# A hybrid recurrent decoder layer: the samples' queries times their states in four array columns side by side, the residual's norm moved into the second MLP product, and a third weight buffer

## The chip, the cores and the metric

One core of one Trainium2 chip runs the whole layer. The metric is the device time of one execution in microseconds. Three runs of the kernel before took 936.66, 937.22 and 938.57 us; the median is 937.22 us.

## The reference

One layer is applied to a prompt of 512 tokens and to eight samples of four tokens each, with shared weights; together they are 544 token columns. The kernel keeps activations transposed: a channel is a partition, a token a column.

```
proj = x @ w_in + b_in                       # 1024 -> 51 blocks of 128 channels
GLA:   S_t = diag(exp g_t) S_{t-1} + k_t^T v_t,  o_t = q_t S_t,   RMS norm per head, times silu(gr)
mLSTM: C_t = f C_{t-1} + i k_t v_t^T,  n_t likewise,  h_t = q_t C_t / max(|q_t . n_t|, 1),  layer norm per head
HGRN2: the same scan as GLA, with its own gate
merged = sum over branches of sigmoid(mg) * (h_branch @ w_up)
x = LayerNorm(ALPHA * x + merged @ w_out)
x = LayerNorm(ALPHA * x + square(relu(x @ w_ff_up)) @ w_ff_down)
```

The prompt starts from zero states. Each sample starts from a state that is given (for GLA and HGRN2 four heads of 48 x 96 or 64 x 64, for mLSTM four heads of 96 x 97 with n as the last column), so each sample needs its queries times its state, and its updated state goes out.

## The kernel before, in words

**Dense products.** Every dense product goes through `gemm` (L162): one block of 128 output channels by 544 tokens. A float32 weight tile `raw` is loaded on SP's queue (three buffers, L137); `wload` then splits it on ScalarE into a rounded high half `wh` (L141) and on VectorE into the rest `wl` (L142), two buffers each. `mm` (L158) issues, for each block of 128 input channels, three products (high by high, high by low, low by high) in two halves of 272 tokens: six matmuls. A product with 1024 input channels has 48 matmuls, `wup_ml` and `wup_gla` have 18, `wup_hg` 12. Its result is in one of two PSUM buffers `g` and is read by one VectorE instruction.

**Order.** A scheduler places all instructions of the program on the engines' in-order queues by a simulated time; `tc.high_priority` moves some forward. The order on each engine is therefore fixed in the built program, and the scans are mixed with the dense products: projection blocks, mLSTM (five chunks, the samples among them), GLA scan, mLSTM's merge, HGRN2 scan, the other merges, `wout` with the first norm, and the MLP in two halves of 16 hidden blocks.

**The samples' products.** In `gated` (GLA and HGRN2) `sample` makes the output transposed, `oT` (value channels by tokens). Four matmuls add the part within the four tokens (L498). For each pair of heads p and each sample n, one matmul has the state `Ss[:, n]` (128 x 96 or 128 x 64) as the stationary operand and eight columns of queries `qx` as the moving one (L509): 16 in GLA, 16 in HGRN2. They carry a lowered priority (`BEHIND`), so the scheduler puts them between other matmuls. The result is copied by ScalarE (L525), turned by four transposes (L528) and normed by `rms_rows`. In `ml_chunk(4)` the same is done for mLSTM: for each head eight matmuls with the state `Cs[:, n]` (96 x 97) stationary and four columns of queries moving (L770), 32 in all, then a copy (L781), four transposes (L784) and a copy into `num` (L785). After its products a state is scaled and updated in place (L517 to L519; L772 to L777) and stored.

A float32 matmul is two MATMUL records in the trace, each with a weight load of its own; the rounded `fp32r` ones of the dense products are one.

**The residual's norm.** The first layer norm leaves the sums `ne` (minus the mean) and `rstd` (L990 to L999); the first MLP product takes the centred but not yet normed rows and corrects its result by `ne` and `rstd` (L1037, L1038), then applies relu and square on ScalarE and splits the hidden block into high and low (L180). The residual itself, `x1`, is normed during the first 16 hidden blocks: for block m the loop issues one VectorE instruction on row block m // 2, an add of `ne` (L1052) for even m, a multiply by `rstd` (L1054) for odd m, and then an affine step on ScalarE (L1055). The second product of the first half adds its result to ALPHA times that row block.

**The last merge** (`Merge` with `wup_hg`, 2 input blocks): for each of eight output blocks a gate product of 48 matmuls is followed by an up product of 12.

Of the kernel before, what the change touches and what calls it, by code (L numbers as in the profile page):

```python
# [27 lines left out]
BEHIND = 380  # L28
# [15 lines left out]
def build(tc, I, O):  # L44
    nc = tc.nc
    with ExitStack() as ctx:
# [85 lines left out]

        def wload(src, nk):

            n = nk * 128
            raw = wp.tile([128, 1024], F32, tag="raw", name="raw", bufs=3)
            nc.sync.dma_start(out=raw[:, 0:n], in_=src)  # L137
            h = wp.tile([128, 1024], F32R, tag="wh", name="wh")
            l = wp.tile([128, 1024], F32R, tag="wl", name="wl")
            with tc.high_priority(OFF):  # L140
                nc.scalar.activation(out=h[:, 0:n], in_=raw[:, 0:n], func=AF.Copy)  # L141
                nc.vector.tensor_tensor(out=l[:, 0:n], in0=raw[:, 0:n], in1=h[:, 0:n].bitcast(F32), op=ALU.subtract)  # L142
            return h, l
# [207 lines left out]
        def gated(q, k, b, sc, dv, vtok, sname, nt, gate):  # L351
# [5 lines left out]
            def levels(u):  # L357
# [85 lines left out]
                qx = t1.tile([128, 2, 8, 2, 4], F32, tag="qx", name="qx", bufs=1)  # L443
                nc.gpsimd.memset(qx, 0.0)
                for e in range(2):
                    s = slice(64 * e, 64 * e + 64)
                    nc.vector.tensor_tensor(
                        out=qx[s, :, :, e, :], in0=qv[s].rearrange("p a (n m) -> p a n m", m=4),
                        in1=P[s, :, 0:32].rearrange("p a (n m) -> p a n m", m=4), op=ALU.mult)
# [44 lines left out]
            def sample():  # L494
                at, P, qx, k3 = (st[2][n] for n in ("at", "P", "qx", "k3"))
                oT = psr.tile([128, 512], F32, tag="r", name="oTs")
                for h in range(4):
                    nc.tensor.matmul(oT[0:dv, h * 32:(h + 1) * 32], vtok[0:32, 4, h * dv:(h + 1) * dv], at[0:32, h, 0:32],  # L498
                                     start=(h == 0), stop=False)
                v3 = stack_v(vtok[0:32, 4, 0:d4], d4)  # L500
                nb = 512 // dv // 4 * 4
                yield
                for p in range(2):
                    Ss = t1.tile([128, 8, 97], F32, tag="Ss", name="Ss")
                    nc.scalar.dma_start(out=Ss[:, :, 0:dv], in_=I[sname][p])
                    for n in range(8):

                        with tc.high_priority(-(BEHIND + 4 * n)):
                            nc.tensor.matmul(  # L509
                                oT[0:dv, p * 64:(p + 1) * 64].rearrange("p (a b) -> p a b", a=2)[:, :, 4 * n:4 * n + 4],  # L510
                                Ss[:, n, 0:dv], qx[:, p, n], start=False, stop=(p == 1 and n == 7))
# [12 lines left out]
                oTs = t1.tile([97, 128], F32, tag="oTs", name="oTsb", bufs=1)  # L524
                nc.scalar.activation(out=oTs[0:dv], in_=oT[0:dv, 0:128], func=AF.Copy)  # L525
                o = psr.tile([128, 512], F32, tag="r", name="osm")
                for h in range(4):
                    nc.tensor.transpose(o[0:32, h * dv:(h + 1) * dv], oTs[0:dv, h * 32:(h + 1) * 32], ident[0:dv, 0:dv])  # L528
                on = rms_rows(32, o[0:32, 0:d4].rearrange("p (a b) -> p a b", a=4), dv)
                yield  # L530
                finish_rows(32, on, nt, gate, TP)
# [161 lines left out]
        def ml_chunk(c):  # L693
# [53 lines left out]
            else:  # L747
# [4 lines left out]
                for h in range(4):  # L752
                    nc.vector.tensor_tensor(out=qF[h], in0=ip[0:96, h * 32:(h + 1) * 32], in1=qF[h], op=ALU.mult)
                ca = t1.tile([96, 4, 8], F32, tag="cas", name="cas", bufs=1)
                nc.vector.tensor_copy(ca[:, :, :, None], ip[0:96, 0:128].rearrange("p (h n m) -> p h n m", h=4, m=4)[:, :, :, 3:4])
                oT = psr.tile([128, 512], F32, tag="r", name="oTm")
                for h in range(4):
                    nc.tensor.matmul(oT[0:97, h * 32:(h + 1) * 32], mvt[0:32, 4, h, :], A[0:32, h * 32:(h + 1) * 32], start=(h == 0), stop=False)
# [5 lines left out]
                for h in range(4):  # L764
# [4 lines left out]
                    for n in range(8):  # L769
                        nc.tensor.matmul(oT[0:97, h * 32 + 4 * n:h * 32 + 4 * n + 4], Cs[:, n, :], qF[h][:, 4 * n:4 * n + 4],  # L770
                                         start=False, stop=(h == 3 and n == 7))
# [8 lines left out]
                oTs = t1.tile([97, 128], F32, tag="oTs", name="oTm", bufs=1)  # L780
                nc.scalar.activation(out=oTs, in_=oT[0:97, 0:128], func=AF.Copy)  # L781
                op = psr.tile([128, 512], F32, tag="r", name="opm")
                for h in range(4):
                    nc.tensor.transpose(op[0:32, h * 97:(h + 1) * 97], oTs[:, h * 32:(h + 1) * 32], ident[0:97, 0:97])  # L784
                nc.vector.tensor_copy(num[0:32], h4(op[0:32, 0:388], 97))  # L785
# [25 lines left out]
        mls.close()  # L811

# [76 lines left out]
        merged = mgp.tile([128, KD, T], F32, name="merged")  # L889
        mm_ = Merge(1, mgate, 3, "wup_ml", first=True)  # L890
# [137 lines left out]
        for blk in range(2):  # L1028
            hid = []
            deep = [hl3("hdh", "hh"), hl3("hdl", "hl")] + [w6.tile([128, 3 * T], F32R, tag="w6", name="hdw").rearrange("p (a b) -> p a b", a=3) for i in range(2)]  # L1030
            for m in range(16):
# [16 lines left out]
                if blk == 0:  # L1048

                    y = x1[:, m // 2, :]  # L1050
                    if m % 2 == 0:
                        nc.vector.tensor_tensor(out=y, in0=y, in1=ne, op=ALU.add)  # L1052
                    else:
                        nc.vector.tensor_tensor(out=y, in0=y, in1=rstd, op=ALU.mult)  # L1054
# [62 lines left out]
        hls.close()  # L1117
        gbs.close()
# [117 lines left out]
```

## Time and profile before

| what | before |
|---|---|
| time of the profiled execution | 937.23 us |
| its span, from first to last instruction | 935.1 us |
| median of three runs | 937.22 us |
| TensorE busy | 915.1 us (98%), 7271 matmul records |
| VectorE busy | 570.4 us (61%) |
| ScalarE busy | 436.9 us (47%) |
| GpSimd busy | 46.8 us (5%) |
| granted TensorE clock | 0.995 |

Some 2.1 us of the profiled time lie outside the span. The profile is one execution on the chip. A busy TensorE is one that has a matmul under way; since matmuls overlap, the time between the starts of two tells more than the duration of one. In a timeline row the first column is the start in us, the second the length of the merged piece, and x8 counts the records in it; a matmul's shape is given as stationary (128\*96) and moving (128x8). "idle before" is the time in which the engine did nothing, with the instruction that ended it. The chain of waits follows the execution back from its last instruction, at each step to what released it.

### The profile page before, as it was taken

To read this page: it belongs to the slowest core of one execution; us is meant where nothing else is said; L and a number is where in the kernel's file an instruction comes from. 1 tells how busy PE (TensorE), PEld (TensorE's weight loads), DVE (VectorE), ACT (ScalarE), POOL (GpSimd) and SP (SyncE) were. 2 spreads that over 40 slices of the span, in tenths; PEclk is the share of its full clock that TensorE was granted. 3 is DMA by queue.
4 is the path that set the end of the run, shared out by engine and by line. 5 is a ranking of instruction groups with operands and counts; after the bars stand their busy time and mean duration, and the time that the engine had idled before them with its cause. 6 is when DMAs were issued, how large, how long until landed. Compare 5 with 4: busy or idle time off the path is not lost.

```text
span 935.1 us, 17425 instructions
## 1 busy us (share of the span) xinstructions
PE 915.1 (98%) x7271; PEld 897.1 (96%) x7271; DVE 570.4 (61%) x995; ACT 436.9 (47%) x822; POOL 46.8 (5%) x62
## 2 busy tenths in 40 slices
PE   9999999999999999999999989999999999999995
PEld 7998999999999989999999989999999999999994
DVE  5886468867877658785558695553222455545345
ACT  5395222975536755535444375542111355432215
POOL 1302130001001001000000000000000000000000
PEclk9999999999999999999999999999999999999998
DMA  7321232123122113023235222222222222322302
GB/s 265 122 71 66 72 114 73 37 82 100 63 93 94 54 29 119 27 79 107 68 118 149 99 71 88 91 91 90 91 86 79 86 91 91 91 90 81 100 23 96
DMA packets 37598, 82.73 MB, mean 88 GB/s; under 512 B 12708, under 2 KB 18340, under 8 KB 37520
## 3 DMA queue, kind: packets, MB, share of 16 engines
q1 hardware_dynamic: 25072, 73.28, 24.1%
q10 hardware_dynamic: 12384, 8.33, 3.1%
q8 instruction: 57, 0.93, 0.4%
q14 instruction: 21, 0.17, 0.1%
q0 software_dynamic: 64, 0.02, 0.0%
HBM read 76.51 MB, written 5.09 MB: 87 GB/s over the span
## 4 chain that ended last, share of the span: by engine, by line
PE 93%; DVE 4%; ACT 2%; DMA 1%; issue 1%; ACTq 0%; DVEq 0%
PE g L158 79%; PE lv L410 3%; PE g L84 3%; DVE wl L142 1%; PE o L467 1%; PE qkp L682 1%; PE oTs L509 1%; ACT wh L141 1%; PE oTm L770 1%; DVE merged L1054 1%; PE oT L286 0%; PE vt L259 0%; PE o L470 0%; DMA fw<-in_wfirst 0%; DVE merged L1052 0%
## 5 line engine op out<-in xcount | busy, mean ns | idle before, releaser
L141 ACT ACTIVATE wh<-raw 128x1024 fp32r<-128x1024 f32 (+2 forms) x139 | 133.3, 959 | 231.9 <-PE g L158 199.4
L142 DVE TENSOR_TENSOR wl<-raw,wh 128x1024 fp32r<-128x1024 f32 (+2 forms) x139 | 155.2, 1117 | 134.9 <-ACT wh L141 133.1
L158 PE MATMUL g<-xh,wl 128*128 128x272 f32 x752 | 161.9, 293 | 1.2 <-DVE wl L142 1.2
L158 PE MATMUL g<-xh,wh 128*128 128x272 f32 x752 | 161.0, 293 | 0.3 <-DVE z L833 0.3
L158 PE MATMUL g<-xl,wh 128*128 128x272 f32 x752 | 160.8, 292 | 0.0
L158 PEld LDWEIGHTS g<-xh,wl 128*128 128x128 f32 x752 | 119.4, 189 | 2.9 <-DVE wl L142 2.5
L158 PEld LDWEIGHTS g<-xh,wh 128*128 128x128 f32 x752 | 119.6, 189 | 1.5 <-DVE z L833 0.5
L158 PEld LDWEIGHTS g<-xl,wh 128*128 128x128 f32 x752 | 119.4, 189 | 1.0 <-issue 0.5
L158 PE MATMUL g<-x1h,wh 128*128 128x272 f32 (+1 forms) x512 | 106.5, 289 | 2.8 <-DVE relu L1037 2.8
L158 PE MATMUL g<-x1l,wh 128*128 128x272 f32 (+1 forms) x512 | 106.5, 289 | 0.0
L158 PE MATMUL g<-x1h,wl 128*128 128x272 f32 (+1 forms) x512 | 106.3, 289 | 0.0
L158 PEld LDWEIGHTS g<-x1h,wh 128*128 128x128 f32 x512 | 80.9, 189 | 3.3 <-DVE relu L1037 3.2
L158 PEld LDWEIGHTS g<-x1l,wh 128*128 128x128 f32 x512 | 81.2, 189 | 0.1
L158 PEld LDWEIGHTS g<-x1h,wl 128*128 128x128 f32 x512 | 80.9, 189 | 0.0
L1039 ACT ACTIVATE relu<-relu,gw 128x544 f32<-128x544 f32 x32 | 24.0, 750 | 73.8 <-DVE relu L1038 73.8
L158 PE MATMUL g<-hidh,wh 128*128 128x272 f32 x280 | 58.1, 288 | 0.0
L158 PE MATMUL g<-hidl,wh 128*128 128x272 f32 x280 | 58.1, 289 | 0.0
L158 PE MATMUL g<-hidh,wl 128*128 128x272 f32 x280 | 57.9, 288 | 0.0
L158 PEld LDWEIGHTS g<-hidh,wl 128*128 128x128 f32 x280 | 43.9, 188 | 0.1
L158 PEld LDWEIGHTS g<-hidl,wh 128*128 128x128 f32 x280 | 43.9, 188 | 0.0
L158 PEld LDWEIGHTS g<-hidh,wh 128*128 128x128 f32 x280 | 43.8, 188 | 0.0
L215 DVE TENSOR_SCALAR gb<-g,vec 128x544 f32<-128x544 f32 x24 | 18.8, 783 | 31.5 <-PE g L158 31.3
(398 smaller groups left out, 1661.0 us busy)
## 6 DMA issues: line engine op xcount, KB each, us to landing
raw<-in_wff SPq DMA_DIRECT2D x64, 512.0 KB, 3.5
raw<-in_win SPq DMA_DIRECT2D x47, 512.0 KB, 3.2
xr<-in_xT SPq DMA_DIRECT2D x16, 272.0 KB, 3.4
raw<-in_wout SPq DMA_DIRECT2D x8, 512.0 KB, 3.7
out_yT<-merged SPq DMA_DIRECT2D x8, 272.0 KB, 2.2
fw<-in_wfirst ACTq DMA_DIRECT2D x8, 256.0 KB, 5.4
raw<-in_wup_ml SPq DMA_DIRECT2D x8, 192.0 KB, 2.3
raw<-in_wup_gla SPq DMA_DIRECT2D x8, 192.0 KB, 2.3
```

What stands on the lines that cost most here:

```text
L84: nc.tensor.matmul(first_ps[i][hf], w[:, i * 128:(i + 1) * 128], a[:, k, hf * HT:(hf + 1) * HT], start=(k == 0 and n == 0), stop=(k == KD ...
L141: nc.scalar.activation(out=h[:, 0:n], in_=raw[:, 0:n], func=AF.Copy)
L142: nc.vector.tensor_tensor(out=l[:, 0:n], in0=raw[:, 0:n], in1=h[:, 0:n].bitcast(F32), op=ALU.subtract)
L158: nc.tensor.matmul(ps[:, hf, 0:w_], w, a(k)[:, hf * HT:hf * HT + w_], start=(k == 0 and s == 0), stop=(k == nk - 1 and s == 2))
L215: nc.vector.tensor_scalar(out, ps, vcol(col), XMIN, ALU.add, ALU.max)
L410: nc.tensor.matmul(lv[0:R, o:o + 2 * H].rearrange("p (a b) -> p a b", a=2), Kv[:, p, c * R:(c + 1) * R], Q[:, p, :, c * H:(c + 1) * H], st ...
L467: nc.tensor.matmul(o[:, h * dv:(h + 1) * dv], at[:, c * 4 + h, :], vtok[:, cc, h * dv:(h + 1) * dv], start=(h == 0), stop=(cc == 0 and h = ...
L509: nc.tensor.matmul(oT[0:dv, p * 64:(p + 1) * 64].rearrange("p (a b) -> p a b", a=2)[:, :, 4 * n:4 * n + 4], Ss[:, n, 0:dv], qx[:, p, n], s ...
L682: nc.tensor.matmul(ps[0:96, hf, 0:HT], w[:, i, h, :], a[h][:, hf * HT:(hf + 1) * HT], start=(n == 0), stop=(n == 2))
L770: nc.tensor.matmul(oT[0:97, h * 32 + 4 * n:h * 32 + 4 * n + 4], Cs[:, n, :], qF[h][:, 4 * n:4 * n + 4], start=False, stop=(h == 3 and n == 7))
L1039: nc.scalar.activation(out=r_, in_=r_, func=AF.Relu, bias=gw[:, 1:2])
L1054: nc.vector.tensor_tensor(out=y, in0=y, in1=rstd, op=ALU.mult)
```

## The change

Three things are changed.

1. **The samples' products.** The operands are exchanged: the queries are stationary and the state is the moving operand. For GLA and HGRN2 `qx` holds for each pair of heads and each sample a block of 32 columns, zero but for the eight of this sample (two heads by four tokens, at a place that depends on whether the sample's number is even or odd); sample n = 2j + i writes to PSUM partitions 32j to 32j + 31, that is to a quarter j of the array's columns, and the two samples of a quarter are added there. In each group of eight matmuls the four quarters follow each other. mLSTM does the same with `qz`, 32 columns per sample of which four are filled, one group of eight per head. The number of these matmuls stays (16, 16 and 32); the order numbers and the lowered priority `BEHIND` are gone. The part within the four tokens now has the attention block stationary (32 x 32) and the values moving (L504, L771 of the new file), four matmuls as before, into a PSUM tile of its own that is copied at once. The result no longer needs transposes. Instead ScalarE copies it to SBUF (`oxs`), small DMAs on SP's queue bring each quarter's eight rows together (`orow`: four copies for mLSTM, eight for GLA, eight for HGRN2), and one VectorE add joins the two parts.
2. **The residual's norm.** It is taken out of the loop over hidden blocks. Before each of the eight second products of the first half, two VectorE instructions and one on ScalarE now make the normed row block in a tile of its own, `xn` (one buffer), which the product's result is added to.
3. **A third weight buffer.** From mLSTM's merge on, every third weight tile takes `wh` and `wl` from a second pool with one buffer of each (`w3`).

```diff
+        more_w, nload = [], [0]
         def wload(src, nk):
...
-            h = wp.tile([128, 1024], F32R, tag="wh", name="wh")
-            l = wp.tile([128, 1024], F32R, tag="wl", name="wl")
+            w_ = more_w[0] if more_w and nload[0] % 3 == 2 else wp
+            nload[0] += 1
+            h = w_.tile([128, 1024], F32R, tag="wh", name="wh")
+            l = w_.tile([128, 1024], F32R, tag="wl", name="wl")
...
-                oT = psr.tile([128, 512], F32, tag="r", name="oTs")
+                ol = psr.tile([128, 512], F32, tag="r", name="ol")
                 for h in range(4):
-                    nc.tensor.matmul(oT[0:dv, h * 32:(h + 1) * 32], vtok[0:32, 4, h * dv:(h + 1) * dv], at[0:32, h, 0:32],
-                                     start=(h == 0), stop=False)
+                    nc.tensor.matmul(ol[0:32, h * dv:(h + 1) * dv], at[0:32, h, 0:32], vtok[0:32, 4, h * dv:(h + 1) * dv],
+                                     start=(h == 0), stop=(h == 3))
+                os_ = tile2([32, d4], "os")
+                nc.scalar.activation(out=os_, in_=ol[0:32, 0:d4], func=AF.Copy)
...
-                    for n in range(8):
-                        with tc.high_priority(-(BEHIND + 4 * n)):
-                            nc.tensor.matmul(
-                                oT[0:dv, p * 64:(p + 1) * 64].rearrange("p (a b) -> p a b", a=2)[:, :, 4 * n:4 * n + 4],
-                                Ss[:, n, 0:dv], qx[:, p, n], start=False, stop=(p == 1 and n == 7))
+                    for i in range(2):
+                        for j in range(4):
+                            nc.tensor.matmul(ox[32 * j:32 * j + 32, p * dv:(p + 1) * dv], qx[:, p, j, i], Ss[:, 2 * j + i, 0:dv],
+                                             start=(p == 0 and i == 0), stop=(p == 1 and i == 1))
...
-                oTs = t1.tile([97, 128], F32, tag="oTs", name="oTsb", bufs=1)
-                nc.scalar.activation(out=oTs[0:dv], in_=oT[0:dv, 0:128], func=AF.Copy)
-                o = psr.tile([128, 512], F32, tag="r", name="osm")
-                for h in range(4):
-                    nc.tensor.transpose(o[0:32, h * dv:(h + 1) * dv], oTs[0:dv, h * 32:(h + 1) * 32], ident[0:dv, 0:dv])
-                on = rms_rows(32, o[0:32, 0:d4].rearrange("p (a b) -> p a b", a=4), dv)
+                oxs, orow = tile2([128, 2 * dv], "oxs"), tile2([32, d4], "orow")
+                nc.scalar.activation(out=oxs, in_=ox[:, 0:2 * dv], func=AF.Copy)
+                for j in range(4):
+                    for e in range(2):
+                        nc.sync.dma_start(out=orow[8 * j:8 * j + 8].rearrange("t (p e d) -> t p e d", p=2, e=2)[:, :, e],
+                                          in_=oxs[32 * j + 8 * e:32 * j + 8 * e + 8].rearrange("t (p d) -> t p d", p=2))
+                nc.vector.tensor_tensor(out=os_, in0=os_, in1=orow, op=ALU.add)
+                on = rms_rows(32, os_.rearrange("p (a b) -> p a b", a=4), dv)
...
-                    for n in range(8):
-                        nc.tensor.matmul(oT[0:97, h * 32 + 4 * n:h * 32 + 4 * n + 4], Cs[:, n, :], qF[h][:, 4 * n:4 * n + 4],
-                                         start=False, stop=(h == 3 and n == 7))
+                    z = qz[:, h % 2]
+                    nc.vector.tensor_copy(z.rearrange("p (n t) -> p n t", t=36)[:, :, 0:4], qF[h].rearrange("p (n m) -> p n m", m=4))
+                    for i in range(2):
+                        for j in range(4):
+                            n = 2 * j + i
+                            nc.tensor.matmul(ox[32 * j:32 * j + 32, h * 97:(h + 1) * 97], z[:, 32 * n:32 * n + 32], Cs[:, n, :],
+                                             start=(h == 0 and i == 0), stop=(h == 3 and i == 1))
...
+        w3s, w3p = pool("w3")
...
+        more_w.append(w3p)
         mm_ = Merge(1, mgate, 3, "wup_ml", first=True)
...
-                if blk == 0:
-                    y = x1[:, m // 2, :]
-                    if m % 2 == 0:
-                        nc.vector.tensor_tensor(out=y, in0=y, in1=ne, op=ALU.add)
-                    else:
-                        nc.vector.tensor_tensor(out=y, in0=y, in1=rstd, op=ALU.mult)
-                        nc.scalar.activation(out=y, in_=y, func=AF.Identity, scale=vcol(V_L1G + m // 2), bias=vcol(V_L1B + m // 2))
...
+                if blk == 0:
+                    xn = fp.tile([128, T], F32, tag="xn", name="xn", bufs=1)
+                    nc.vector.tensor_tensor(out=xn, in0=x1[:, m, :], in1=ne, op=ALU.add)
+                    nc.vector.tensor_tensor(out=xn, in0=xn, in1=rstd, op=ALU.mult)
+                    nc.scalar.activation(out=xn, in_=xn, func=AF.Identity, scale=vcol(V_L1G + m), bias=vcol(V_L1B + m))
                 ps = gemm([(w[:, 0:1024], 8), (w[:, 1024:2048], 8)], hh_, hl_)
...
-                    nc.vector.scalar_tensor_tensor(xm, xm, ALPHA, ps, ALU.mult, ALU.add)
+                    nc.vector.scalar_tensor_tensor(xm, halves(xn), ALPHA, ps, ALU.mult, ALU.add)
```

Since the scheduler places everything anew, the order changes in other parts too. Three places show it; the names are the tiles of the program.

On TensorE, at the start of the samples' part of the HGRN2 scan, the built program before has these rows (`lv` is an attention level of the prompt, `g` a dense product, `oTs` the samples' products, `kvs` a state update):

```order
L410 MATMUL lv<-qe_3863,ke_3861 128x128 x4
L509 MATMUL oTs<-qx,Ss 64x2x4 x2
L410 MATMUL lv<-qe_3862,ke_3860 128x128 x4
L158 MATMUL g<-xh,wl 128x272 x2
L509 MATMUL oTs<-qx,Ss 64x2x4
L158 MATMUL g<-xh,wh 128x272 x2
L158 MATMUL g<-xl,wh 128x272 x2
L509 MATMUL oTs<-qx,Ss 64x2x4
L158 MATMUL g<-xh,wl 128x272 x2
L517 MATMUL kvs<-vx,k_3915 128x512
```

and the changed program has, at the same place (`ox` is the samples' products now):

```order
L413 MATMUL lv<-qe_3884,ke_3882 128x128 x4
L518 MATMUL ox<-Ss,qx 32x64 x9
L413 MATMUL lv<-qe_3883,ke_3881 128x128 x4
L525 MATMUL kvs<-vx,k_3938 128x512
L518 MATMUL ox<-Ss,qx 32x64 x7
L161 MATMUL g<-xh,wl 128x272
```

The sixteen products, which stood in fifteen places, one or two at each, stand in two.

On VectorE, around the end of the first layer norm, before (`rstd` is its last sum, `wl` the low half of a weight tile, `relu` reads the product's result out of PSUM):

```order
L996 TENSOR_TENSOR rstd<-m_6319,rstd 128x272
L1052 TENSOR_TENSOR merged<-merged,ne 128x544 x8
L142 TENSOR_TENSOR wl<-raw,wh 128x1024
L1037 SCALAR_TENSOR_TENSOR relu<-ne,gw,g 128x544
L1054 TENSOR_TENSOR merged<-merged,rstd 128x544 x8
L142 TENSOR_TENSOR wl<-raw,wh 128x1024
```

and now:

```order
L1018 TENSOR_TENSOR rstd<-m_6350,rstd 128x272
L1076 TENSOR_TENSOR xn<-merged,ne 128x544
L145 TENSOR_TENSOR wl<-raw,wh 128x1024
L1059 SCALAR_TENSOR_TENSOR relu<-ne,gw,g 128x544
L1077 TENSOR_TENSOR xn<-xn,rstd 128x544
L1060 TENSOR_TENSOR relu<-relu,rstd 128x544
L145 TENSOR_TENSOR wl<-raw,wh 128x1024
```

Of the eight adds ahead of the first `relu` and the eight multiplies behind it, one of each is left there.

On SP's queue, in the GLA scan's part, the weight loads now have the small copies of rows between them:

```order
L138 DMA raw<-in_wup_ml 128x384 x2
L536 DMA orow<-oxs 8x2x96 x7
L138 DMA raw<-in_wup_ml 128x384
L536 DMA orow<-oxs 8x2x96
L138 DMA raw<-in_wup_ml 128x384
L138 DMA raw<-in_win 128x1024 x12
```

and VectorE's queue has, up to the add that reads these rows (`merged`, `gb` and `wl` belong to the dense products, `Ss` is the state's update):

```order
L218 TENSOR_SCALAR gb<-g,vec 128x544
L145 TENSOR_TENSOR wl<-raw,wh 128x1024
L417 COPY_PREDICATED at<-lmask,lv 128x64x8
L398 TENSOR_TENSOR ke_2109<-kg,E 128x128x2
L405 TENSOR_TENSOR qe_2111<-qg,E 64x2x128 x2
L417 COPY_PREDICATED at<-lmask,lv 128x128x4
L527 SCALAR_TENSOR_TENSOR Ss<-Ss,P,kvs 128x96 x4
L538 TENSOR_TENSOR os<-os,orow 32x384
L527 SCALAR_TENSOR_TENSOR Ss<-Ss,P,kvs 128x96 x4
L218 TENSOR_SCALAR gb<-g,vec 128x544
```

Before there were the weight loads alone on SP; the last of the eight copies stands behind one more weight load. That load takes the `raw` buffer that the `wl` of the second row here sets free.

More of the change, by code (lines that the diff above doesn't have):

```diff
@@ L27 @@
 OFF = 1000000
-BEHIND = 380
 NF = 4
@@ L442, in levels @@
                 st[u].update(at=at, P=P)
-                qx = t1.tile([128, 2, 8, 2, 4], F32, tag="qx", name="qx", bufs=1)
+                qx = t1.tile([128, 576], F32, tag="qx", name="qx", bufs=1)[:, 0:512].rearrange("p (a j i c) -> p a j i c", a=2, j=4, i=2)
                 nc.gpsimd.memset(qx, 0.0)
+                n4 = lambda a: a.rearrange("p a (j i m) -> p a j i m", i=2, m=4)
                 for e in range(2):
                     s = slice(64 * e, 64 * e + 64)
-                    nc.vector.tensor_tensor(
-                        out=qx[s, :, :, e, :], in0=qv[s].rearrange("p a (n m) -> p a n m", m=4),
-                        in1=P[s, :, 0:32].rearrange("p a (n m) -> p a n m", m=4), op=ALU.mult)
+                    for i in range(2):
+                        nc.vector.tensor_tensor(
+                            out=qx[s, :, :, i, 8 * e + 4 * i:8 * e + 4 * i + 4], in0=n4(qv[s])[:, :, :, i],
+                            in1=n4(P[s, :, 0:32])[:, :, :, i], op=ALU.mult)
                 k3 = t1.tile([96, 2, 2, 128], F32R, tag="k3", name="k3", bufs=1)
@@ L502, in sample @@
                 yield
+                ox = psr.tile([128, 512], F32, tag="r", name="ox")
                 for p in range(2):
@@ L753, in ml_chunk @@
                     nc.vector.tensor_tensor(out=qF[h], in0=ip[0:96, h * 32:(h + 1) * 32], in1=qF[h], op=ALU.mult)
+                qz = t1.tile([128, 576], F32, tag="qx", name="qz", bufs=1)[0:96].rearrange("p (a b) -> p a b", a=2)
+                nc.gpsimd.memset(qz, 0.0)
                 ca = t1.tile([96, 4, 8], F32, tag="cas", name="cas", bufs=1)
                 nc.vector.tensor_copy(ca[:, :, :, None], ip[0:96, 0:128].rearrange("p (h n m) -> p h n m", h=4, m=4)[:, :, :, 3:4])
-                oT = psr.tile([128, 512], F32, tag="r", name="oTm")
+                ol = psr.tile([128, 512], F32, tag="r", name="ol")
                 for h in range(4):
-                    nc.tensor.matmul(oT[0:97, h * 32:(h + 1) * 32], mvt[0:32, 4, h, :], A[0:32, h * 32:(h + 1) * 32], start=(h == 0), stop=False)
+                    nc.tensor.matmul(ol[0:32, h * 97:(h + 1) * 97], A[0:32, h * 32:(h + 1) * 32], mvt[0:32, 4, h, :], start=(h == 0), stop=(h == 3))
+                nc.vector.tensor_copy(num[0:32], h4(ol[0:32, 0:388], 97))
+                ox = psr.tile([128, 512], F32, tag="r", name="oxm")
                 k3 = t1.tile([96, 4, 96], F32R, tag="k3", name="k3m", bufs=1)
@@ L768, in ml_chunk @@
                     nc.scalar.dma_start(out=Cs, in_=I["mC"][h])
-                    for n in range(8):
-                        nc.tensor.matmul(oT[0:97, h * 32 + 4 * n:h * 32 + 4 * n + 4], Cs[:, n, :], qF[h][:, 4 * n:4 * n + 4],
-                                         start=False, stop=(h == 3 and n == 7))
+                    z = qz[:, h % 2]
+                    nc.vector.tensor_copy(z.rearrange("p (n t) -> p n t", t=36)[:, :, 0:4], qF[h].rearrange("p (n m) -> p n m", m=4))
+                    for i in range(2):
+                        for j in range(4):
+                            n = 2 * j + i
+                            nc.tensor.matmul(ox[32 * j:32 * j + 32, h * 97:(h + 1) * 97], z[:, 32 * n:32 * n + 32], Cs[:, n, :],
+                                             start=(h == 0 and i == 0), stop=(h == 3 and i == 1))
                     vx = spread_v(v3[:, h * 97:(h + 1) * 97], 97)
@@ L779, in ml_chunk @@
                 yield
[L780 to L785, printed above, removed]
+                oxs, orow = tile2([128, 388], "oxsm"), tile2([32, 388], "orowm")
+                nc.scalar.activation(out=oxs, in_=ox[:, 0:388], func=AF.Copy)
+                for j in range(4):
+                    nc.sync.dma_start(out=orow[8 * j:8 * j + 8], in_=oxs[40 * j:40 * j + 8])
+                nc.vector.tensor_tensor(out=num[0:32], in0=num[0:32], in1=h4(orow, 97), op=ALU.add)
             yield
@@ L811, in build @@
         mls.close()
+        w3s, w3p = pool("w3")
+        pass
         def open_kq():
@@ L1117, in build @@
         hls.close()
+        w3s.close()
         gbs.close()
```

## The prediction, made before the changed kernel was run

> **What bounds the kernel now.** I read the page first, then TensorE's busy time by stretches, then the waits of TensorE.
>
> ```profile
> span 935.1 us, 17425 instructions
> PE 915.1 (98%) x7271; PEld 897.1 (96%) x7271; DVE 570.4 (61%) x995; ACT 436.9 (47%) x822; POOL 46.8 (5%) x62
> PE 93%; DVE 4%; ACT 2%; DMA 1%; issue 1%; ACTq 0%; DVEq 0%
> ```
>
> TensorE makes up 93% of the chain that ended last, so a matmul less on TensorE is time less. The stretch of the MLP gives the pace of the dense products:
>
> ```profile
> 600.00:700.00 100.00, 100.00 (x797) 100.00 (x797) 36.85 (x41) 30.64 (x42) 0.00 (x0) 1.00 0.27 85
> ```
>
> 797 records in 100 us are 0.1255 us each, 0.25 for a pair of halves and 6.0 for a product of 48. TensorE's waits are few (us in total, times, longest); the two largest belong to things that the change touches:
>
> ```profile
> PE g L158 <- DVE relu L1037: 2.8, 2, 2.2
> PE g L158 <- DVE wl L142: 1.9, 7, 0.7
> ```
>
> The profiled execution took 937.23 us, span 935.1; the median of the runs shown is 937.22, so what I take off the span I take off the median.
>
> **Part 1: the samples' products, what goes.** All costs are differences of starts on TensorE's timeline. mLSTM, one head's eight products (two records each):
>
> ```profile
> 107.08 1.46 PE L770 MATMUL oTm<-qkf,Cs 96*97 96x4 f32 x16
> 108.39 1.14 PE L699 MATMUL sp<-qkf 96*128 96x128 f32 x8
> ```
>
> 1.31 us a head, 0.082 a record, 5.2 us for four heads. GLA has 18 records in one piece and seven pairs between dense products, such as this one:
>
> ```profile
> 186.17 0.29 PE L158 MATMUL g<-xl,wh 128*128 128x272 f32 x1
> 186.30 0.26 PE L509 MATMUL oTs<-qx,Ss 128*96 128x8 f32 x2
> 186.41 0.37 PE L158 MATMUL g<-xl,wh 128*128 128x272 f32 x1
> 186.62 0.41 PE L158 MATMUL g<-xh,wl 128*128 128x272 f32 x2
> ```
>
> From 186.17 to 186.62 are 0.45 for two dense records (0.25) and a pair, so 0.20 a pair and 1.4 for seven; the 18, with a state as wide as mLSTM's, at its 0.082 are 1.5: 2.9 us. HGRN2's pairs cost twice that, though their stationary operand is narrower:
>
> ```profile
> 330.05 0.52 PE L158 MATMUL g<-xh,wh 128*128 128x272 f32 x2
> 330.40 0.41 PE L158 MATMUL g<-xl,wh 128*128 128x272 f32 x2
> 330.74 0.28 PE L509 MATMUL oTs<-qx,Ss 128*64 128x8 f32 x2
> 330.95 0.52 PE L158 MATMUL g<-xh,wl 128*128 128x272 f32 x2
> ```
>
> The pair itself takes 0.21; the dense pair ahead of it takes 0.34 and the one behind a pair 0.35 (330.05 to 330.40) in place of 0.25. So entering and leaving a matmul of 64 columns costs 0.1 each way, which the 96 columns of GLA did not pay. 0.40 a place; with 15 places, one of them double, 6.1 us. The transposes at the end go too:
>
> ```profile
> L784 PE MATMUL opm<-ident,oTm 97*32 97x97 f32 x4 | 0.5, 248 | 0.0
> L528 PE MATMUL osm<-ident,oTsb 96*32 96x96 f32 x4 | 0.5, 246 | 0.0
> ```
>
> Busy 0.5 us each, and HGRN2's the same at most; less what overlaps with the neighbours, I count 1.2 for the three. The products within the four tokens keep their number and change operands; I count them at nothing (give or take 0.5). Together 15.4 us go.
>
> **Part 1: what comes.** No matmul here uses four column quarters. The nearest is `kvp` of the prompt's scan, whose heads alternate between the two halves of 64 columns, with 96 moving columns like GLA's states. One call of it, first in a window that ends after its first records, then in two that begin later, then whole:
>
> ```profile
> 225.99 0.28 PE L467 MATMUL o<-gvt,at 128*128 128x96 f32 x1
> 226.20 0.30 PE L475 MATMUL kvp<-gvt,kt 128*64 128x96 f32 x2
> ```
>
> ```profile
> 226.33 0.42 PE L475 MATMUL kvp<-gvt,kt 128*64 128x96 f32 x6
> ```
>
> ```profile
> 226.41 0.34 PE L475 MATMUL kvp<-gvt,kt 128*64 128x96 f32 x4
> ```
>
> ```profile
> 226.20 0.55 PE L475 MATMUL kvp<-gvt,kt 128*64 128x96 f32 x8
> 226.68 0.52 PE L158 MATMUL g<-xl,wh 128*128 128x272 f32 x2
> 227.03 0.42 PE L158 MATMUL g<-xh,wl 128*128 128x272 f32 x2
> ```
>
> The eight records run two by two: two begin at 226.20, two at 226.33, two at 226.41. They do share the array, in rounds of 0.08 after a first one of 0.13. The call takes 0.48 until the next dense record; leaving costs 0.10 (0.35 in place of 0.25), entering 0.10 (0.21 from the `o` record before to the first one; I put an `o` record alone at 0.11, an estimate from the 0.93 that eight of them take to the next call in the fence below). So four rounds with entry and exit cost 0.68. For HGRN2's 64 moving columns:
>
> ```profile
> 367.98 1.00 PE L467 MATMUL o<-hvt,at 128*128 128x64 f32 x8
> 368.91 0.45 PE L475 MATMUL kvp<-hvt,kt 128*64 128x64 f32 x8
> 369.29 0.52 PE L158 MATMUL g<-xh,wh 128*128 128x272 f32 x2
> 369.65 0.41 PE L158 MATMUL g<-xl,wh 128*128 128x272 f32 x2
> ```
>
> 0.38 + 0.11 + 0.10 = 0.59. If four quarters run side by side as two halves do, a new group of eight products (16 records) is four rounds as well. In the built order mLSTM has four groups, two of them cut in two by other matmuls (0.3 more each): 4 x 0.68 + 0.6 = 3.3; GLA two, 1.4; HGRN2 two, 1.2. Together 5.9. The bounds: eight rounds, if only two run at a time, add 4 x 0.08 in six groups and 4 x 0.05 in two, 2.3 us; sixteen, if none do, add three times that, 7.0. Below 5.9 there is only what entry and exit cost, about 1.6 us. I take 5.9, since it is the row with the same operand type and the same alternation. **Part 1 gains 15.4 - 5.9 = 9.5 us.**
>
> A rule against it: the Trainium skill (TensorE: Matmul & The Clock Gate, Measured speedup vs the span model) gives 2.38 times for three column tiles, 79% of three. By that the 2.8 us of rounds in the 5.9 would be 3.5 and the time 0.7 us longer. The rows above show two halves at an even 0.08 a round; no run here shows three or four.
>
> The rest of part 1 lies beside TensorE: the copies on ScalarE (47% busy), the adds and small `qx` and `qz` writes on VectorE (61%), larger clears on GpSimd (5%). What they delay is the sums at the end of a scan, whose results the merges need some products later. If that cover were gone, a whole chain of copy, DMA and norm would be exposed, about 5 us per scan. The twenty small copies on SP are a rival, below.
>
> **Part 2: the residual's norm.** The first of the two waits in the row above, 2.8 us in total and 2.2 the longer, is at the start of the MLP. What VectorE does there, from the chain of waits:
>
> ```profile
> 544.53 5.08 DVE merged L1054 x8
> ```
>
> Both PSUM buffers were full because `relu` stood behind eight adds and then behind eight multiplies (5.08 us for these, 0.64 each; an add is of the same kind and size). In the new order one add and one multiply remain there. The first `relu` comes seven adds, 4.5 us, earlier, more than the 2.2 waited; the second likewise. Gain 2.8 us of idle time and 0.1 at each restart (the 0.35 for a pair after a pause, as at 226.68): **3.0**. The 16 instructions move beside second products of 96 matmuls (12 us each), where VectorE was 37% busy in the row of 600 to 700 us; no cost. Should `xn` be late, a product's result waits in PSUM, and there are two buffers. Bounds: none of the 3.0, or all; below, nothing.
>
> **Part 3: the third weight buffer.** In the last merge the chain leaves TensorE in each round:
>
> ```profile
> 446.28 5.56 PE g L158 x42
> ...
> 451.86 1.07 ACT wh L141
> ...
> 452.95 1.24 DVE wl L142
> ...
> 454.23 5.56 PE g L158 x42
> ...
> 479.01 1.12 DVE wl L142
> ```
>
> A gate's weights can only be split when the gate product before it has freed their buffer; the split takes 1.07 + 1.24 = 2.3 us, and the up product that covers it has 12 matmuls, 1.5 us. A round lasts 7.95 (446.28 to 454.23) where 60 matmuls need 7.53. Five of the seven waits for `wl` in the row at the top are such rounds: 5 x 0.42 = 2.1. The longest, 0.7 and a restart, is at the first product of `wout` (479.01), whose weights follow the last up product in the same way: 0.8. With a third buffer the split can start a whole gate product (6.0 us) earlier, and its 2.3 us fit in that; next late would be the gate's own steps, a rival below. **2.9 us.** Elsewhere from mLSTM's merge on TensorE hardly waits for weights, so no more. Bounds 0 and 3.4.
>
> **Sum.** 9.5 + 3.0 + 2.9 = 15.4 off 937.2 gives 921.8. A new order brings waits of its own, and others of the old order go. I put both together at about nothing and say **921.5 us**; its own range is 918 to 924.
>
> **Rivals.**
> - *The quarters don't run side by side as the halves do.* For: no row has four. Against: the pairs above. 2.3 or 7.0 us more: 924 or 928.5. Chance 0.14.
> - *The third buffer changes nothing,* because the chain then hangs on the gate's own steps (evacuation, three ScalarE steps, multiply, add, split). For: the same order of instructions on VectorE and ScalarE. Against: TensorE never waits for anything but `wl` there. 924.4. Chance 0.08.
> - *Blocked adds, slower.* The add of `orow` waits for copies on SP, and the last stands behind a weight load that waits for a `raw` buffer. If it reaches the head of VectorE's queue first, the evacuation of `g` and the next `wl` stand behind it. Cover is the other PSUM buffer, one product of 6.0 us; the wait has to exceed that. Late by a further product each, three adds cost 3 x 6.0 = 18 us: 939.5. Against: the `wl` that frees that buffer stands six instructions ahead of the add, and a copy between SBUF rows lands in 3 us even from GpSimd's queue:
>
> ```profile
> rli<-qg POOLq DMA_DIRECT2D x1, 8.5 KB, 2.9
> ```
>
> Chance 0.05.
> - *More goes than I count:* entry and exit of quarters cheaper, waits of the old order gone. 917. Chance 0.08.
>
> **How the numbers follow.** The forecast has the remaining 0.65. The range 915.5 to 928.5 holds it and the rivals but the slower one and the far ends of the others. About 0.2% (1.9 us) is what a measurement of this kernel can tell from no change; only the blocked adds, wholly or in part, come near it: faster 0.94, same 0.02, slower 0.04.
>
> **What would show it.** Right: records of `ox` and `oxm` starting four by four, a group of 16 in 0.5 us; no wait for `relu` L1059 over 0.5 us after the first norm; rounds of the last merge of 7.5 us; no wait of the add of `orow` that TensorE feels. Wrong: rounds of `ox` one or two at a time; rounds of the merge still at 7.9; or TensorE idle behind `gb` or `wl` right after an add of `orow`.

## The result, and the profile after

The changed kernel takes **927.5 us** in the median of four runs (925.94 to 927.73), the kernel before 937.84 (four runs, 936.66 to 938.57): a ratio of 0.9887, interval 0.987 to 0.9905. That is 10.6 us less by the ratio (8.9 to 12.2), where 15.7 were forecast. The profiled execution took 925.94 us, 11.3 less than that of before. It lies inside the range on record and outside the forecast's own range of 918 to 924.

The page of the changed kernel: span, busy times, chain.

```profile
span 923.9 us, 17471 instructions
PE 902.7 (98%) x7259; PEld 885.9 (96%) x7259; DVE 573.9 (62%) x1006; ACT 437.8 (47%) x824; POOL 49.8 (5%) x63
PE 95%; DVE 2%; ACT 2%; DMA 0%; issue 0%; ACTq 0%; DVEq 0%
```

TensorE is busy 12.4 us less, and its share of the chain rises from 93% to 95%. Its waits (total, times, longest):

```profile
PE oT L289 <- DVE on L303: 2.6, 1, 2.6
PE g L161 <- ACT hh L182: 1.9, 1, 1.9
PE g L161 <- DVE qh L218: 1.4, 1, 1.4
```

The two waits that the change was aimed at, `relu` (2.8) and `wl` (1.9), are gone, and three that the kernel before did not have stand in their place: for `on`, a chunk's normed output, which the transposes `oT` turn; for `hh`, the rounded half of HGRN2's gated output; and for `qh`, HGRN2's queries, which VectorE reads out of a PSUM buffer `g`. Two are at the end of the GLA scan, one (`hh`) at the end of the HGRN2 scan. TensorE's timeline at the first place; the last column gives the idle time before an instruction and what ended it:

```profile
280.23 0.52 PE L476 MATMUL o<-S,Qt 128*128 128x192 f32 x2
283.33 0.52 PE L289 MATMUL oT<-ident,on 128*128 128x128 f32 x3 [2.59 <-DVE on L303]
...
285.33 0.55 PE L481 MATMUL kvp<-gvt,kt 128*64 128x96 f32 x8
287.32 0.52 PE L161 MATMUL g<-xh,wh 128*128 128x272 f32 x2 [1.44 <-DVE qh L218]
```

TensorE stands at the transposes of a chunk whose norm is still being made, and no dense matmul lies between the chunk's last `o` and them. Then it stands again, because both PSUM buffers hold products of HGRN2's queries. What VectorE did meanwhile:

```profile
278.91 1.23 DVE L145 TENSOR_TENSOR wl<-raw,wh 128x1024 fp32r<-128x1024 f32 x1 [0.17 <-ACT wh L144]
280.06 1.39 DVE L489 SCALAR_TENSOR_TENSOR S<-S,P,kvp 64x96 f32<-64x96 f32 x4
281.48 0.55 DVE L299 TENSOR_REDUCE ss<-sq 128x4 f32<-128x384 f32 x1
282.63 0.56 DVE L303 TENSOR_TENSOR on<-o,ss 128x384 f32<-128x384 f32 x1 [0.60 <-ACT ss L301]
283.89 0.56 DVE L291 TENSOR_TENSOR ggate<-oT,ggate 128x384 f32<-128x384 f32 x1 [0.70 <-PE oT L289]
286.02 0.55 DVE L299 TENSOR_REDUCE ss<-sq 128x4 f32<-128x384 f32 x1 [1.57 <-ACT sq L297]
286.49 1.47 DVE L218 TENSOR_SCALAR qh<-g,vec 128x544 f32<-128x544 f32 x2
```

The evacuation `qh` (L218) stands in the queue behind the second chunk's `ss`, which waits for that chunk's `o` on TensorE, which stands behind the transposes: one late norm is paid twice. At the end of the HGRN2 scan, TensorE's rows and ScalarE's:

```profile
419.10 0.38 PE L289 MATMUL oT<-ident,on 128*128 128x128 f32 x2
421.38 0.39 PE L161 MATMUL g<-hh,wh 128*128 128x272 f32 x1 [1.89 <-ACT hh L182]
```

```profile
420.12 0.66 ACT L209 ACTIVATE gb<-gb 128x544 f32<-128x544 f32 x1 [0.66 <-DVE gb L218]
420.69 0.64 ACT L182 ACTIVATE hh<-hgate 128x544 fp32r<-128x544 f32 x1
```

An up product stands right behind the last transposes and needs their result gated and split. With the restarts, the three places cost 2.7, 1.6 and 2.1 us (starts against the usual distance of the same pair of instructions), and two smaller ones (`o` at 278.29 behind `at`, `vt` at 300.38) 0.5 and 0.4 more: 7.3 us. The order of before had waits of its own that are gone now, for `qe` (0.9 with its restart) and for mLSTM's `Cs` (0.6).

The new groups of samples' products, a whole one and one that is cut in two:

```profile
107.83 0.28 PE L161 MATMUL g<-xh,wh 128*128 128x272 f32 x1
108.04 0.54 PE L790 MATMUL oxm<-Cs,qz 96*32 96x97 f32 x16
108.51 0.42 PE L796 MATMUL kvs<-vx,k3m 96*96 96x388 f32 x1
...
118.94 0.37 PE L790 MATMUL oxm<-Cs,qz 96*32 96x97 f32 x6
119.24 1.13 PE L734 MATMUL na<-mvt,D 128*128 128x97 f32 x8
120.31 0.52 PE L790 MATMUL oxm<-Cs,qz 96*32 96x97 f32 x10
120.76 0.39 PE L161 MATMUL g<-xh,wh 128*128 128x272 f32 x1
```

Sixteen records take 0.47 us from their first start to the next instruction's; in the trace four start within 0.02 us, the next four 0.11 later, then 0.08 and 0.09.

Where the time went, place by place, is read from two starts on TensorE's timeline: the first record of the MLP (`x1h`) and the first of its second product (`hidh`). Before, then after:

```profile
528.27 0.29 PE L158 MATMUL g<-x1h,wh 128*128 128x272 f32 x1
...
634.92 0.29 PE L158 MATMUL g<-hidh,wh 128*128 128x272 f32 x1
```

```profile
519.96 0.29 PE L161 MATMUL g<-x1h,wh 128*128 128x272 f32 x1
...
623.25 0.29 PE L161 MATMUL g<-hidh,wh 128*128 128x272 f32 x1
```

Up to the MLP 8.3 us were gained, from there to the second product another 3.4, and behind it 0.5 lost.

### The profile page after: what moved, and what is told of

Its sections match the earlier page's. It is cut to its first block, busy times and chain, and to the rows that moved or that the text cites. A ratio compares the mean times of both kernels' runs of the same rounds, so it can differ in the third digit from the quotient of the medians.

```text
span 923.9 us, 17471 instructions
## 1 busy us (share of the span) xinstructions
PE 902.7 (98%) x7259; PEld 885.9 (96%) x7259; DVE 573.9 (62%) x1006; ACT 437.8 (47%) x824; POOL 49.8 (5%) x63
## 4 chain that ended last, share of the span: by engine, by line
PE 95%; DVE 2%; ACT 2%; DMA 0%; issue 0%; ACTq 0%; DVEq 0%
PE g L161 82%; PE lv L413 3%; PE g L83 3%; PE o L473 1%; PE qkp L692 1%; PE vt L262 0%; PE oT L289 0%; DMA fw<-in_wfirst 0%; PE o L476 0%; PE m L1008 0%; PE na L734 0%; ACT merged L1131 0%; PE dps L372 0%; PE sp L709 0%; PE kvp L481 0%
## 5 line engine op out<-in xcount | busy, mean ns | idle before, releaser
L161 PE MATMUL g<-xl,wh 128*128 128x272 f32 x752 | 157.5, 290 | 0.0
L161 PE MATMUL g<-x1l,wh 128*128 128x272 f32 (+1 forms) x512 | 106.7, 289 | 0.0
L161 PE MATMUL g<-hdw,wh 128*128 128x272 f32 x168 | 34.9, 289 | 0.0
```

Of the source, the lines that this page charges most:

```text
L161: nc.tensor.matmul(ps[:, hf, 0:w_], w, a(k)[:, hf * HT:hf * HT + w_], start=(k == 0 and s == 0), stop=(k == nk - 1 and s == 2))
```

## The experiments

Two theories at the start. *A*: each of the three parts gains what its term said, and the missing 5 us are waits that the order of all three together brings. *B*: one of the terms was too large. *C*, put down for the run with the buffer alone and kept from there on: the third weight buffer by itself brings these waits.

All ratios are against runs of the kernel before on the same chip; differences in us are such a ratio times 937.8.

### Each part alone

The kernel before with only the hunks of one part of the diff.

> The kernel before with part 1 alone (the samples' products in column quarters); norm and weight buffers as before. Theory A (each part gains what its term says, the missing 6 us are waits that the new order of all three together brings): 9.5 us less, about 928.3. Rival B (part 1 itself is the mis-sized term: TensorE time saved inside the GLA scan has no dense products to be filled with): 4 to 6 us less, 932 to 934. In both the groups of 16 records cost 0.6 to 0.75 us each.

> The kernel before with part 2 alone (the residual's norm in the second product). Theory A: the wait for relu (2.8 us) goes, 3.0 us less, about 934.8. Rival B (the norm only moves the wait): under 1 us less.

> The kernel before with part 3 alone (the third weight buffer). Theory A: the waits for wl (1.9 us) and their restarts go, 2.9 us less, about 934.9. Rival C (the buffer lets dense products run ahead until they fill both PSUM buffers before the end of the GLA scan, so that TensorE is idle there): wl waits go as well, but idle of 3 to 5 us appears at the end of the GLA scan and the time is within 2 us of before or longer.

| part | median us | ratio (interval) | difference us | forecast | MLP starts | second product starts |
|---|---|---|---|---|---|---|
| samples' products | 926.9 | 0.9884 (0.9869 to 0.9899) | -10.9 | -9.5 | 517.41 | 624.78 |
| norm | 932.73 | 0.9948 (0.9933 to 0.9963) | -4.9 | -3.0 | 528.88 | 631.96 |
| third buffer | 938.17 | 1.0005 (0.9994 to 1.0016) | +0.5 | -2.9 | 529.29 | 635.93 |

Parts 1 and 2 gain at least what was forecast. The third buffer alone gains nothing. TensorE's largest waits in its run:

```profile
PE g L162 <- DVE relu L1044: 2.8, 2, 2.2
PE g L162 <- ACT hh L183: 1.9, 1, 1.9
PE g L162 <- ACT W L431: 1.5, 1, 1.5
```

No wait for `wl` is left, so the buffer does what it is for, but `hh` (at the end of the HGRN2 scan, 430.7) and `W` (in the GLA scan, 214) have come in. B falls for parts 1 and 2; C's price (3.4 us of waits, and the time of before) is right, though it had expected them at the end of the GLA scan.

### Order changed, nothing else

The changed kernel with two edits.

```diff
-            for j in range(nt):
-                nc.tensor.transpose(ps[:, j * r:(j + 1) * r], ...
+            with tc.high_priority(-200):
+                for j in range(nt):
+                    nc.tensor.transpose(ps[:, j * r:(j + 1) * r], ...
...
-        mr_.gates(0, gbp, 1)
+        mr_.gates(0, gbp, 2)
         mr_.split()
         for m in range(KD):
-            if m + 1 < KD:
-                mr_.gates(m + 1, gbp, 1)
+            if m + 2 < KD:
+                mr_.gates(m + 2, gbp, 1)
```

> The changed kernel with two edits to the order alone: the transposes that end a chunk's scan get a lower priority (200 back), and the last merge computes two gates ahead instead of one. Theory A (the missing time is TensorE behind the transposes of the norm chain at the end of the GLA scan, 4.9 us, and behind the split of hgate at the end of the HGRN2 scan, 2.1 us): 4 to 7 us less than the changed kernel, 920.5 to 923.5. Rival B (the terms were mis-sized, the waits stand for work that had to wait anyway): within 1.5 us of the changed kernel's 927.5.

924.75 us, ratio 0.9855 (0.9838 to 0.9871): 3 less than the changed kernel by the ratios, less than A wanted and more than B did. The wait for `hh` is gone. The one at the end of the GLA scan is not:

```profile
PE oT L290 <- DVE on L304: 3.2, 1, 3.2
PE dp L717 <- POOL rd L715: 1.0, 1, 1.0
```

A lower priority of the transposes does not cure it, and another wait (`dp`) has come. One of mLSTM's cut groups is whole here and GLA's two stand together, worth 1.0 us by TensorE's starts. Each build brings an order of its own; the 3 us agree with 2.1 for `hh` and 1.0 for the groups, the other changes (`qh` 0.9 less, `on` 0.6 and `dp` 1.0 more, the two smaller waits gone) nearly balance, and the run settles no more.

### Without the buffer, with it late, with it early

The changed kernel with one line gone (`more_w.append(w3p)`); with this line moved to the last merge, behind `mr_ = Merge(2, ...)`; to GLA's merge, behind `mg_ = Merge(0, ...)`; and with the line in its place and `more_w.clear()` behind `mr_ = ...`, so that the buffer serves only up to the last merge. The last two as diffs:

```diff
-        more_w.append(w3p)
...
         mg_ = Merge(0, ggate, 3, "wup_gla")
+        more_w.append(w3p)
```

```diff
         mr_ = Merge(2, hgate, 2, "wup_hg", fin=(mh, ml))
+        more_w.clear()
```

> The changed kernel without part 3: the third weight buffer is reserved but never used; samples' products and norm as changed. Theory A (the third buffer is worth 2.9 us here too): 1.5 to 3 us more than the changed kernel, about 930. Theory C (as the run of the buffer alone suggests: what the third buffer takes off TensorE's waits for wl it gives back at the ends of the GLA and HGRN2 scans, because the order built with it runs dense products earlier): the waits for on, qh and hh at the two ends go, those for wl come back; the gains of parts 1 and 2 measured alone, 10.9 and 5.1, then add up: 921.8, and in any case not above the changed kernel.

> The changed kernel with the third weight buffer used only from the last merge on (the up products of HGRN2, wout, the MLP), after both scans' ends. Theory C: the ends of the scans look as without the buffer, the waits for wl in the last merge are gone, 2 to 3 us less than the kernel with two parts, 919 to 920. Theory A: same as the changed kernel or up to 1 us more.

> The changed kernel with the third weight buffer used only from GLA's merge on: after the end of the GLA scan, but through the end of the HGRN2 scan. Theory C, told by place: TensorE waits for neither on nor qh at the end of the GLA scan (as without the buffer), and still waits 1 to 2 us for hh at the end of the HGRN2 scan, since one row of an up product stands there right behind the last transposes; 921 to 923, between 920.1 (buffer from the last merge on) and 927.5 (changed kernel). Theory A: the time of the changed kernel, 926 to 928.

> The changed kernel with the third weight buffer used only up to the last merge, the complement of the run with the late buffer. Theory C: all of what the buffer costs and none of what it gains: the waits for on (2.6 us), qh (1.4) and hh (1.9) at the ends of the scans as in the changed kernel, and the waits for wl in the last merge back; 928.5 to 931, 1 to 3.5 us more than the changed kernel and 5 to 7 more than without the buffer. Theory A: the kernel without the buffer, 923, or less.

| third buffer used | median us | ratio (interval) | difference us | MLP starts |
|---|---|---|---|---|
| never | 923.05 | 0.9845 (0.9832 to 0.9859) | -14.5 | 517.48 |
| from the last merge on | 920.11 | 0.9809 (0.9796 to 0.9823) | -17.9 | 515.01 |
| from GLA's merge on | 920.72 | 0.9832 (0.981 to 0.9853) | -15.8 | 514.53 |
| from mLSTM's merge on (the change) | 927.5 | 0.9887 (0.987 to 0.9905) | -10.6 | 519.96 |
| from mLSTM's to the last merge | 928.54 | 0.9914 (0.9896 to 0.9933) | -8.1 | 522.52 |

Without the buffer the kernel is faster than with it, against theory A. Used late the buffer gains 3.4 us by the ratios; used early alone it costs 6.5. These two, -14.5 - 3.4 + 6.5 = -11.4, give the changed kernel's -10.6 within the intervals. The best version, the buffer from the last merge on, beats both kernels: 920.11, below even the forecast for the changed kernel. C's own figures (921.8, 919 to 920, 921 to 923, 928.5 to 931) came out right in the last and up to 1.3 us beside in the others.

The traces make the loss smaller than the ratios do. From the first `oxm` record to the MLP's first they give 409.49 us without the buffer, 406.16 with it from the last merge on, 406.63 from GLA's merge on, 413.73 up to the last merge and 411.92 in the changed kernel. Used late it gains 3.3 there, as by the ratios; used early alone it costs 4.2, not 6.5, partly because it also takes away waits that the kernel without it has (`wh` 0.7, `wl` 0.3 and 0.3), and the late use on top of that gains only 1.8. So the sign of the early loss is sure and its size lies between about 4 and 6.5 us. Nearly all of it comes with the use from mLSTM's merge to GLA's. In the MLP, where TensorE hardly waits, the buffer costs a little: from its first record to the end of the span are 404.0 us in all eight kernels with parts 1 and 2 that use it there, 403.4 in the two that don't. The reason for that was not looked for.

The kernel without the buffer at the end of the GLA scan:

```profile
276.52 0.54 PE L481 MATMUL kvp<-gvt,kt 128*64 128x96 f32 x6
277.00 0.39 PE L161 MATMUL g<-xl,wh 128*128 128x272 f32 x1
...
281.00 0.42 PE L161 MATMUL g<-xh,wl 128*128 128x272 f32 x2
281.25 0.49 PE L289 MATMUL oT<-ident,on 128*128 128x128 f32 x3
```

4.2 us of dense matmuls stand between the chunk's last matrices and its transposes, long enough for the norm. In both kernels the same 1632 matmuls of dense products have run before the scan's last `kvp`; the changed kernel had finished them by 278.3, ahead of these `o`, and its next one waited for `qh`. Of that wait 0.6 us are left here (the changed kernel has 1.4). So the amount of cover is the same, and its place is not. With the buffer used early only, the same waits as in the changed kernel are there to the tenth, and those for `wl` are back:

```profile
PE oT L289 <- DVE on L303: 2.6, 1, 2.6
PE g L161 <- DVE wl L145: 2.1, 7, 0.7
PE g L161 <- ACT hh L182: 1.9, 1, 1.9
PE g L161 <- DVE qh L218: 1.4, 1, 1.4
```

From GLA's merge on, `on` is gone, `qh` is 0.6 where none was expected, and `hh` is 0.8 where 1 to 2 were.

The waits belong to the order that a build makes, and the buffer makes such orders likely, not certain. Of the fourteen kernels here (both, and the twelve runs), seven use it from mLSTM's merge on, and five of these wait for `on` at the end of the GLA scan; the buffer alone and the run with one quarter (below) don't. Of the seven others none does. For `hh` 0.8 or more are waited by seven of the eight that use the buffer at the end of the HGRN2 scan, all but the one that computes two gates ahead, and by none of the other six. Why the scheduler spends its dense products earlier when it has a third buffer was not tried; that weights which are ready sooner let it do so is an argument only.

One more run put the lower priority of the transposes on the version with the late buffer:

> The kernel with the third buffer from the last merge on, and the transposes that end a chunk's scan at a lower priority. Theory C: no wait at the scans' ends is left for this to take away; GLA's two groups of samples' products become one of 32 records (0.4 us less) and one cut of mLSTM's goes (0.6 less): 919 to 920.5. If the lower priority was by itself what made the run of the two edits of order faster than the changed kernel by 2.8, 917 to 918.

921.1 us, ratio 0.984 (0.9813 to 0.9868): no better, as C says, though C had 919 to 920.5. GLA's group is one of 32 records, and a new wait for `wl` of 1.8 us inside the GLA scan (ended at 250.7) takes back what that gives.

### The quarters

Three runs on the samples' groups, the changed kernel with another order of a group's products, or with all of them in one quarter. The last mixes the samples' sums, so only its times say something.

```diff
-                    for i in range(2):
-                        for j in range(4):
+                    for j in range(4):
+                        for i in range(2):
...
+PAIRS = [(0, 0), (0, 1), (1, 0), (1, 1), (0, 2), (0, 3), (1, 2), (1, 3)]
+                    for i, j in PAIRS:
...
-nc.tensor.matmul(ox[32 * j:32 * j + 32, h * 97:(h + 1) * 97], ...
+nc.tensor.matmul(ox[0:32, h * 97:(h + 1) * 97], ...
```

> The changed kernel with the two loops of a group of samples' products exchanged, so that the two products of a quarter come one behind the other and then the next quarter's, in place of the four quarters in turn. Theory A (quarters run side by side only if records of other quarters stand next in the queue; the queue is in order): a group of 16 records takes about 0.2 to 0.5 us longer, 1.5 to 4 us in eight groups by TensorE's timeline. Rival D (the four quarters cost nothing of their own, a record alone takes 0.03 us): groups as in the changed kernel, 0.65 to 0.75 us.

> The changed kernel with each group's sixteen records ordered so that only two quarters alternate: quarters 0 and 1 first, then 2 and 3. Theory A: eight rounds of two in place of four of four, 0.3 us more a group of 97 columns and 0.2 more a group of 64, 2.3 us in all by TensorE's timeline. Rival D: no difference.

> The changed kernel with all of a group's sixteen records in the same quarter of the array (the samples' sums are then mixed: this leaves the output of the samples wrong, the work of TensorE the same). By the prediction's bound, sixteen rounds of 0.08 in a group of 97 columns in place of four: about 0.95 us more a group of 16, 1.6 instead of 0.65. If the group takes 0.75 or less, the quarters were never what saved time, only the cheaper record.

The same group of mLSTM quarter by quarter, two at a time, and all in one quarter:

```profile
109.76 0.56 PE L790 MATMUL oxm<-Cs,qz 96*32 96x97 f32 x16
110.25 0.42 PE L796 MATMUL kvs<-vx,k3m 96*96 96x388 f32 x1
```

```profile
107.99 0.56 PE L791 MATMUL oxm<-Cs,qz 96*32 96x97 f32 x16
108.48 0.42 PE L797 MATMUL kvs<-vx,k3m 96*96 96x388 f32 x1
```

```profile
108.08 1.52 PE L790 MATMUL oxm<-Cs,qz 96*32 96x97 f32 x16
109.53 0.59 PE L796 MATMUL kvs<-vx,k3m 96*96 96x388 f32 x2
```

0.49, 0.49 and 1.45 us, against 0.47 in the changed kernel. The order in the queue hardly matters (all groups together 0.3 to 0.4 us more, not 1.5 to 4 or 2.3): where four records of a quarter stand one behind the other, the other quarters' records start all the same. The trace does not name a record's quarter, but it shows that the order did change: quarter by quarter the four of a round start 0.013 us apart, in the changed kernel 0.007; and four of one quarter, one after the other, would take the 0.08 each of the run with one quarter. That the work is spread over four quarters matters: in one quarter a group takes three times as long, and all groups 12.6 us in place of 6.4, 6.2 more where the prediction's bound had 7.0. Rival D falls as well, since a record by itself costs 0.09. The whole times are 929.44, 926.21 and 925.96, one run each. The last is not above the changed kernel's although its groups cost 6.2 us more: its order, again another one, has neither the wait for `on` nor 1.4 for `qh`, and only 0.8 for `hh`.

## Why the prediction was right or wrong

**Part 1, what goes: 15.4; measured 16.9.** By starts on TensorE: mLSTM 6.4 (with 0.6 for a state that came late, which the 1.31 a head left out), GLA 2.9, HGRN2 6.4, transposes 1.2.

**Part 1, what comes: 5.9; measured 6.4.** A whole group with entry and exit costs 0.64 to 0.75 for 96 or 97 columns (0.68 said), HGRN2's 0.65 and 0.59 (0.59 said). The step from two halves to four quarters held: four rounds, four records in each. The cut groups cost 0.5 and 0.6 more, not 0.3. The net gain is 10.5 by TensorE's starts and 10.9 (9.5 to 12.3) in the run alone, against 9.5. The Trainium skill (TensorE: Matmul & The Clock Gate, Measured speedup vs the span model) has 2.38 for three column tiles, 79% of three. Four measured here give 1.45 / 0.47 = 3.1, 77% of four. The trace agrees with that share, for a group that has its leaving in it. The 0.7 us that the rule would have added did not come: the groups came out 0.5 above the 5.9, and the two cuts, 0.2 and 0.3 dearer than said, are all of that. That the copies, adds and `orow` lie beside TensorE held: in the changed kernel nobody waits for the adds of `orow`, and these waited 1.1 and 0.9 us for their copies. The slower rival, blocked adds, did not come.

**Part 2: 3.0; measured 3.4 to 3.6.** From the MLP's first record to its second product before took 106.7 us, after 103.3, the norm alone 103.1. `relu` no longer makes TensorE wait, and `xn` doesn't either. By the run alone it is 4.9 (3.5 to 6.3); its trace does not show what lies above 3.6.

**Part 3: 2.9; measured 3.4 where the step looked, and 6.5 (4.2 by the traces) lost where it didn't.** In the last merge the chain of the changed kernel stays on TensorE:

```profile
439.88 31.50 PE g L161 x251
```

251 matmuls in 31.50 us are 0.1255 each, so a round of 60 takes 7.5, as said. The step's bounds "0 and 3.4" hold for that place alone.

**The step that failed** is the last of the sum: "A new order brings waits of its own, and others of the old order go. I put both together at about nothing." They came to about -1.5 and +7.3, and nearly all of the second, all but 0.7 for `qh`, is absent where only the early use of part 3 is taken away. With the parts as measured the sum is 10.5 (the 0.6 for `Cs` is in it) + 3.4 + 3.4 - 6.5 = 10.8 against 10.6. By the traces alone it is 10.5 + 3.6 for the norm - 4.2 for the early buffer + 1.8 for the late one on top - 0.5 in the MLP = 11.2, as much as the span became shorter. The fault was to read "elsewhere from mLSTM's merge on TensorE hardly waits for weights, so no more" as "so no change": a buffer that nothing waits for can still change when the scheduler issues what it feeds. The rival *the third buffer changes nothing* (924.4) had 2.9 of the 5.1 us that were missed, by a mechanism (the gate's own steps) that the runs do not show; no rival had the mechanism that came. That the time lies inside the range is luck: its upper end was set by quarters that do not run side by side, which they do, and errors of opposite sign helped: parts 1 and 2 gained 1.4 us more than their terms by the trace, 2 by the ratio of the kernel without the buffer.

## What to carry to other kernels

Where a scheduler sets the order, price each part of a change with the ends of the stages at which TensorE depends on a chain of small steps, and look there in the built order for dense work between the last matmul and the transposes that wait for its norm; a buffer can cost there what it gains elsewhere. Give a resource only to the stretch whose wait it removes: the third buffer from the last merge on gave 3.4 us, used from two merges earlier it cost 4 to 6.5 there. And run the parts alone before their sum is believed, for parts that add up on TensorE's timeline do not add up in the order.

## What the runs showed of the hardware

Records of different column quarters do not have to alternate in the queue to run side by side: with four of one quarter in a row a group took 0.49 us against 0.47, and in one quarter 1.45. Entering and leaving such a group costs about 0.08 and 0.10 us (0.21 from 107.83 to 108.04 where the dense records are 0.125 apart, and 0.23 from the first dense record behind, at 120.76, to the next), one reason why a group cut in two costs 0.5 to 0.6 more.
